# First-block modulation by blocks of 128 weight columns in a two-block transformer kernel

## The chip, the cores and the metric

The kernel runs on one core of one Trainium2 chip. The metric is the device time of one execution in microseconds (us); less is better. Engines are called as the profile calls them: PE (TensorE matmuls), PEld (its weight loads), DVE (VectorE), ACT (ScalarE), POOL (GpSimd) and SP (SyncE, which here only issues transfers).

## The reference, cut to what matters

All inputs are float32. The change touches only the modulation at the head of the first block: two vectors (c for the 1024 tokens of x, c_ctx for the 256 tokens of ctx) go through silu and one matrix of 1024 x 3072, and the result scales, shifts and gates.

```python
mod   = silu(c)     @ w_mod + b_mod          # (1, 3072): shift, scale, gate
mod_c = silu(c_ctx) @ w_mod + b_mod
h  = rms(x,   norm_g) * (1 + scale)   + shift      # 1024 x 1024
hc = rms(ctx, norm_g) * (1 + scale_c) + shift_c    #  256 x 1024
u  = h @ w_in;  uc = hc @ w_in    # parts: cq (256), ckv (128), kr (64), ga, pin, gp (512 each)
...                               # attention, pooling, gates
x = x + gate * (branches @ w_out)
```

The second block (retention and gated linear attention, a dense feed-forward, HGRN2, a mixture of eight experts) follows and is untouched.

## The kernel before

Activations lie transposed, 128 features on the partitions and tokens along the free axis, so the model width of 1024 is eight blocks k. Precise float32 products are made of split operands: a value is a high part `h` (float32r) and a low part `l`, and `mm3` (L214 to L222) issues three matmuls for a product, `wh*xh`, `wh*xl`, `wl*xh`.

Weights come through the class `Weights`. `add` writes an entry into a plan; `get` is called in the order of the plan, loads some entries ahead (`_load`, L108 to L114, one transfer of up to 512 KB into one of four `wraw` buffers, issued on SP or, later, on ACT) and splits up to two ahead (`_split`, L116 to L133: an ACT copy gives `wh`, L130, a DVE subtraction gives `wl`, L131; three pairs of buffers). The order of instructions on each engine is made at build time by a scheduler that goes by the order of the program and by what is ready in its own estimate of time; the engines then run their queues in order.

`first` works in this order. The small vectors are loaded and transposed, silu is taken of c and c_ctx, and `sc` holds the two results split into high and low parts (four columns for each k, L296 to L301). Ten tiles of x and ctx are loaded, transposed on PE (L317) and copied (L320), with their sums of squares (L312); the scale of each token is spread over the partitions by ten float32 products with the identity (L329). Then the modulation: `mod_products` (L372 to L379) takes, for each k and each of the parts shift and scale, the 128 rows of w_mod that belong to k (4 KB in a row, 512 KB in all), with `sc` as the stationary operand (four columns) and the weights moving, 512 columns at a time, high and then low: 64 matmuls into four banks, whose sums are complete only after k = 7. `modulation` (L381 to L396) copies the four rows out (L387), turns them into columns with 16 small transposes (L390) and adds the bias. Only then can the loop over k at L347 start. For each k DVE and ACT make the operands `hch`, `hcl`, `hxh`, `hxl` (L353 to L355) and PE adds the products of this k for ckv and kr: 18 matmuls in six open banks, called a dense step below. After k = 7 ACT drains the banks (L361) and `prep` goes on with cq and pin.

The third part (gate) is taken later, in `branches`: after each of four projections `gp` (48 matmuls each) come the products of two k (8 matmuls each pair of k, 32 in all), and after the last, `modulation` and a copy to `modg` (L689). Attention follows.

Of the kernel before, what the change touches and what calls it, by code (L numbers as in the profile page):

```python
# [10 lines left out]
F32 = mybir.dt.float32  # L11
F32R = mybir.dt.float32r
I32 = mybir.dt.int32
U8 = mybir.dt.uint8
AF = mybir.ActivationFunctionType
OP = mybir.AluOpType
# [5 lines left out]
D = 1024  # L22
NK = 8
HALF = 512
# [70 lines left out]
class Weights:  # L95
# [7 lines left out]
        self.plan, self.loaded, self.ready = [], [], []  # L103
        self.at = 0

    def add(self, key, src, k, m, dup=False):
        self.plan.append((key, src, k, m, dup))

    def _load(self, i):
        key, src, k, m, dup = self.plan[i]  # L110
        t = self.raw.tile([128, 1024], F32, name="wraw", tag="wraw")
        v = t[:, :k * m].rearrange("p (k m) -> p k m", k=k)
        self.queue.dma_start(v, src)
        self.loaded.append(v)  # L114

    def _split(self, i):  # L116
        key, src, k, m, dup = self.plan[i]
        v = self.loaded[i]
        w = 2 * m if dup else m
        h = self.pair.tile([128, 1024], F32R, name="wh", tag="wh")  # L120
        l = self.pair.tile([128, 1024], F32R, name="wl", tag="wl")
        hv = h[:, :k * w].rearrange("p (k m) -> p k m", k=k)
        lv = l[:, :k * w].rearrange("p (k m) -> p k m", k=k)
        if dup:
            for s in range(2):
                self.nc.scalar.activation(hv[:, :, s * m:(s + 1) * m], v, AF.Copy)
                self.nc.vector.tensor_tensor(lv[:, :, s * m:(s + 1) * m], v,
                                             hv[:, :, s * m:(s + 1) * m].bitcast(F32), op=OP.subtract)
        else:
            self.nc.scalar.activation(h[:, :k * w], self._flat(v, k, m), AF.Copy)  # L130
            self.nc.vector.tensor_tensor(l[:, :k * w], self._flat(v, k, m), h[:, :k * w].bitcast(F32),  # L131
                                         op=OP.subtract)
        self.loaded[i] = None  # L133
        self.ready.append((hv, lv))
# [33 lines left out]
OFF_CQ, OFF_CKV, OFF_KR, OFF_GA, OFF_PIN, OFF_GP = 0, 256, 384, 448, 960, 1472  # L168


def wsrc(ap, c0, m, k=NK, r0=0):

    row = ap.shape[-1]
    return bass.AP(tensor=ap.tensor, offset=ap.offset + r0 * row + c0, ap=[[row, 128], [128 * row, k], [1, m]])


class Net:
# [74 lines left out]
    def first(s, stop=99):  # L252
        nc, tc, A = s.nc, s.tc, s.A
        s.vectors()
        W = s.W
        wmod, win, wout = A["w_mod"], A["w_in"], A["w_out"]
        def mod_rows(part, k):
            row = wmod.shape[-1]
            W.add(("mod", part, k), bass.AP(tensor=wmod.tensor, offset=wmod.offset + k * 128 * row + part * D,
                                            ap=[[row, 128], [D, 1], [1, D]]), 1, D)  # L260

        for k in range(NK):
            for part in range(2):
                mod_rows(part, k)
        for key, c0, m, dup in (("ckv", OFF_CKV, 128, False), ("kr", OFF_KR, 64, True), ("cq0", 0, 128, False),
                                ("cq1", 128, 128, False)):
            W.add(key, wsrc(win, c0, m), NK, m, dup)
        for nm, off in (("pin", OFF_PIN), ("ga", OFF_GA), ("gp", OFF_GP)):
            for t in range(4):
                W.add((nm, t), wsrc(win, off + t * 128, 128), NK, 128)  # L270
                if nm == "gp":
                    for k in range(2 * t, 2 * t + 2):
                        mod_rows(2, k)
        for t in range(NK):
            W.add(("wout", t), wsrc(wout, t * 128, 128), NK, 128)

# [2 lines left out]
        ckv = early.tile([128, LK], F32, name="ckv")  # L279
        krr = early.tile([128, LK], F32, name="krr")  # L280
        s.modg = s.const.tile([128, NK], F32, name="modg")
        s.sc = s.const.tile([128, NK, 4], F32R, name="sc")
        st = s.pool("start")
        hch = st.tile([128, NK, CTX], F32R, name="hch")
        hcl = st.tile([128, NK, CTX], F32R, name="hcl")
# [7 lines left out]

        cc = s.vt[:, VCOL["c"]:VCOL["c"] + 16].rearrange("p (v k) -> p v k", v=2)

        sl = st.tile([128, 2, NK], F32, name="sl")  # L296
        silu = nc.scalar.activation(sl, cc, AF.Silu)
        s.lnexp(silu.ins)
        scv = s.sc.rearrange("p k (v q) -> p q v k", q=2)
        nc.vector.tensor_copy(scv[:, 0], sl)  # L300
        nc.vector.tensor_tensor(scv[:, 1], sl, scv[:, 0].bitcast(F32), op=OP.subtract)  # L301

        def psS():
            return s.psS.tile([128, HALF], F32, name="s", tag="s")
# [3 lines left out]
        for i in range(10):  # L308
            xr = rp.tile([128, D], F32, name=f"xr{i}")
            src = A["x"][0, i * 128:(i + 1) * 128, :] if i < 8 else A["ctx"][0, (i - 8) * 128:(i - 7) * 128, :]  # L310
            nc.sync.dma_start(xr, src)
            nc.scalar.activation(junk, xr, AF.Square, accum_out=ss[:, i:i + 1])  # L312
            for g in range(2):
                ps = psS()
                for j in range(4):
                    k = g * 4 + j
# [9 lines left out]
        for a, b in ((0, 4), (4, 8), (8, 10)):  # L326
            ps = psS()
            for i in range(a, b):
# [2 lines left out]
            nc.scalar.activation(rb[:, a * 128:b * 128], ps[:, :(b - a) * 128], AF.Copy)  # L331


        acc = s.mod_banks(s.psA, 2)
        s.mod_products(acc, 0, 2, 2, range(NK))
        mod = s.modulation(st, acc, 0, 2, 2)
        A1 = st.tile([128, NK, 2], F32, name="A1")
        nc.vector.scalar_tensor_tensor(A1, mod[:, NK:], 1.0, s.col("norm_g", 0, 8)[:, :, None].to_broadcast([128, NK, 2]),
                                       op0=OP.add, op1=OP.mult)

        nx = ((0, HALF, hxh, hxl, 0, CTX), (1, HALF, hxh, hxl, HALF, CTX + HALF), (2, CTX, hch, hcl, 0, 0))
        todo = []
        for key, dst, pool, nm in (("ckv", ckv, s.psA, "acc"), ("kr", krr, s.psS, "s")):
            w = W.get(key)
            todo += [(w, dst, p, pool.tile([128, HALF], F32, name=nm, tag=nm)) for p in nx]  # L347
        for k in range(NK):
            for src, v, o, dh, dl in ((cT, 1, T, hch, hcl), (xT, 0, 0, hxh, hxl)):
                a1, sh = A1[:, k, v:v + 1], mod[:, k, v:v + 1]  # L350
                n = src.shape[2]
                t = st.tile([128, T], F32, name="xn", tag="xn", bufs=2)[:, :n]
                nc.vector.scalar_tensor_tensor(t, src[:, k, :], a1, rb[:, o:o + n], op0=OP.mult, op1=OP.mult)  # L353
                nc.scalar.activation(dh[:, k, :], t, AF.Identity, bias=sh)
                nc.vector.scalar_tensor_tensor(dl[:, k, :], t, sh, dh[:, k, :].bitcast(F32), op0=OP.add,  # L355
                                               op1=OP.subtract)
            for w, dst, (i, n, xh, xl, o, d0), ps in todo:
                s.mm3(ps[:, :n], w, lambda k: xh[:, k, o:o + n], lambda k: xl[:, k, o:o + n], (k,), first=k == 0,
                      last=k == NK - 1)
# [4 lines left out]
        st.release()  # L364
        s.prep(hxh, hxl, ckv, krr, early, hxp, stop)


    def mod_banks(s, pool, n):
        nm = "acc" if pool is s.psA else "s"
        return [pool.tile([128, HALF], F32, name=nm, tag=nm) for _ in range(2 * n)]  # L370

    def mod_products(s, acc, part, n, nv, kk):  # L372
        for k in kk:
            for j in range(n):
                for i, w in enumerate(s.W.get(("mod", part + j, k))):
                    for h in range(2):
                        s.nc.tensor.matmul(acc[2 * j + h][:2 * nv], s.sc[:, k, :2 * nv],
                                           w[:, 0, h * HALF:(h + 1) * HALF], start=k == 0 and i == 0,
                                           stop=k == NK - 1 and i == 1)  # L379

    def modulation(s, pool, acc, part, n, nv):  # L381

        nc = s.nc
        ps = s.psS.tile([128, HALF], F32, name="s", tag="s")
        for j in range(2 * n):
            rows = pool.tile([4, HALF], F32, name="mrow", tag="mrow", bufs=2)[:2 * nv]
            nc.vector.tensor_copy(rows, acc[j][:2 * nv])  # L387
            for i in range(4):
                o = (j * 4 + i) * 2 * nv
                nc.tensor.transpose(ps[:, o:o + 2 * nv], rows[:, i * 128:(i + 1) * 128], s.ident[:2 * nv, :2 * nv])  # L390
        mod = pool.tile([128, n * NK, nv], F32, name="mod")
        pv = ps[:, :n * NK * 2 * nv].rearrange("p (j v q) -> p j v q", v=nv, q=2)
        nc.vector.tensor_tensor(mod, pv[:, :, :, 0],
                                s.col("b_mod", part * NK, n * NK)[:, :, None].to_broadcast([128, n * NK, nv]), op=OP.add)
        nc.vector.tensor_tensor(mod, pv[:, :, :, 1], mod, op=OP.add)
        return mod  # L396

    def spill(s):
        return s.spp.tile([128, HALF], F32, name="sp", tag="sp", bufs=4)
# [211 lines left out]
    def branches(s, hxh, hxl, hxp, stop):  # L611

        nc, A = s.nc, s.A
        last = s.rs.ins
        bp = s.pool("pool", side="right")
# [66 lines left out]
        s.heads = {}  # L682
        s.apool = [s.pool("attna")]
        s.load_head(0)
        acc = s.mod_banks(s.psS, 1)
        for t in range(4):
            drain(s.proj([("gp", t)], hxh, hxl, lambda i, hf, ps: evac_gp(t, hf, ps)))
            s.mod_products(acc, 2, 1, 1, range(2 * t, 2 * t + 2))
        nc.vector.tensor_copy(s.modg, s.modulation(bp, acc, 2, 1, 1)[:, :, 0])  # L689
        bp.release()  # L690
        hxp.release()
        s.attention(stop)
# [1698 lines left out]
```

## Time and profile before

| | us |
|---|---|
| median of 3 runs | 4607.41 |
| lowest and highest of them | 4606.77, 4609.05 |
| profiled execution, device time | 4609.74 |
| its span, first to last instruction | 4607.9 |
| busy in the span: PE, PEld, DVE, ACT | 4512.7, 3952.9, 2616.4, 1955.9 |

The profile comes from one execution, 2.3 us above the median. Its busy times are unions of spans of instructions; matmuls are pipelined and their ends are modelled, so a difference of starts tells what one costs, and a duration does not. PEclk is the granted clock of TensorE: 1.00 is 2.4 GHz and 0.50 is 1.2 GHz. A view of waits names the engine that waited and what ended the wait.

### The profile page before, as it was taken

To read this page: it belongs to the slowest core of one execution; us is meant where nothing else is said; L and a number is where in the kernel's file an instruction comes from. 1 tells how busy PE (TensorE), PEld (TensorE's weight loads), DVE (VectorE), ACT (ScalarE), POOL (GpSimd) and SP (SyncE) were. 2 spreads that over 40 slices of the span, in tenths; PEclk is the share of its full clock that TensorE was granted. 3 is DMA by queue.
4 is the path that set the end of the run, shared out by engine and by line. 5 is a ranking of instruction groups with operands and counts; after the bars stand their busy time and mean duration, and the time that the engine had idled before them with its cause. 6 is when DMAs were issued, how large, how long until landed. Compare 5 with 4: busy or idle time off the path is not lost. (4 is left out here: it accounts for less than half of the span.)

```text
span 4607.9 us, 67951 instructions
## 1 busy us (share of the span) xinstructions
PE 4512.7 (98%) x28009; PEld 3952.9 (86%) x28010; DVE 2616.4 (57%) x4271; ACT 1955.9 (42%) x3084; POOL 92.2 (2%) x105
## 2 busy tenths in 40 slices
PE   8999999999999999999999899999999999999999
PEld 5668878787888888888886799999999998989897
DVE  6767765666433333577784564545555465655464
ACT  5654543423211111456663344444444444444463
POOL 0001000000000000000000000000000000000000
PEclk9999999999999999999999899999999999999999
DMA  6466231113311111311114555555555555555583
GB/s 218 166 214 162 55 123 37 47 51 120 113 51 42 42 53 51 98 40 40 45 52 135 181 175 186 181 175 184 175 190 180 195 186 208 188 207 192 202 302 124
DMA packets 430497, 620.39 MB, mean 135 GB/s; under 512 B 16784, under 2 KB 211472, under 8 KB 429152
## 3 DMA queue, kind: packets, MB, share of 16 engines
q1 hardware_dynamic: 393360, 555.45, 35.6%
q0 software_dynamic: 20832, 48.83, 3.5%
q10 hardware_dynamic: 15984, 11.66, 0.9%
q8 instruction: 222, 3.64, 0.3%
q14 instruction: 99, 0.81, 0.1%
HBM read 543.08 MB, written 72.88 MB: 134 GB/s over the span
## 5 line engine op out<-in xcount | busy, mean ns | idle before, releaser
L227 DVE TENSOR_TENSOR ml<-mraw,mh 128x1024 fp32r<-128x1024 f32 (+1 forms) x704 | 824.2, 1176 | 758.8 <-ACT mh L226 745.2
L226 ACT ACTIVATE mh<-mraw 128x1024 fp32r<-128x1024 f32 (+1 forms) x704 | 718.3, 1021 | 1073.5 <-PE m L221 798.4
L221 PE MATMUL m<-xl,mh 128*128 128x272 f32 (+1 forms) x3584 | 1025.7, 286 | 0.0
L222 PE MATMUL m<-xh,ml 128*128 128x272 f32 (+1 forms) x3584 | 1024.1, 286 | 0.0
L220 PE MATMUL m<-xh,mh 128*128 128x272 f32 (+1 forms) x3584 | 1020.4, 285 | 1.0 <-ACT mh L226 1.0
L220 PEld LDWEIGHTS m<-xh,mh 128*128 128x128 f32 x3584 | 677.6, 189 | 1.6 <-ACT mh L226 1.3
L222 PEld LDWEIGHTS m<-xh,ml 128*128 128x128 f32 x3584 | 677.9, 189 | 0.2
L221 PEld LDWEIGHTS m<-xl,mh 128*128 128x128 f32 x3584 | 674.1, 188 | 0.3
L130 ACT ACTIVATE wh<-wraw 128x1024 fp32r<-128x1024 f32 (+2 forms) x208 | 203.5, 980 | 597.9 <-PE acc L221 561.1
L131 DVE TENSOR_TENSOR wl<-wraw,wh 128x1024 fp32r<-128x1024 f32 (+2 forms) x208 | 233.1, 1123 | 118.2 <-ACT wh L130 115.3
L220 PE MATMUL acc<-f2h,wh 128*128 128x512 f32 x704 | 274.8, 390 | 0.0
L221 PE MATMUL acc<-f2l,wh 128*128 128x512 f32 x704 | 273.9, 389 | 0.0
L222 PE MATMUL acc<-f2h,wl 128*128 128x512 f32 x704 | 273.9, 389 | 0.0
L220 PE MATMUL m<-hh,mh 128*128 128x272 f32 x896 | 261.0, 291 | 0.0
L222 PE MATMUL m<-hh,ml 128*128 128x272 f32 x896 | 259.9, 290 | 0.0
L221 PE MATMUL m<-hl,mh 128*128 128x272 f32 x896 | 258.9, 289 | 0.0
L2021 PE MATMUL m<-mh,hh 128*128 128x512 f32 x448 | 177.5, 396 | 0.0
L2023 PE MATMUL m<-mh,hl 128*128 128x512 f32 x448 | 177.0, 395 | 0.0
L2022 PE MATMUL m<-ml,hh 128*128 128x512 f32 x448 | 176.5, 394 | 0.0
L220 PEld LDWEIGHTS m<-hh,mh 128*128 128x128 f32 x896 | 168.6, 188 | 0.4
L221 PEld LDWEIGHTS m<-hl,mh 128*128 128x128 f32 x896 | 168.8, 188 | 0.1
L222 PEld LDWEIGHTS m<-hh,ml 128*128 128x128 f32 x896 | 168.5, 188 | 0.2
(559 smaller groups left out, 8940.4 us busy)
## 6 DMA issues: line engine op xcount, KB each, us to landing
mraw<-in_moe_w_up_dram SPq DMA_DIRECT2D x56, 2048.0 KB, 8.6
mraw<-in_moe_w_down_dram SPq DMA_DIRECT2D x64, 1792.0 KB, 7.6
mraw<-in_moe_w_gate_dram SPq DMA_DIRECT2D x55, 2048.0 KB, 8.6
wraw<-in_c_w_in_dram SPq DMA_DIRECT2D x32, 512.0 KB, 4.0
wraw<-in_ab_w_in_dram SPq DMA_DIRECT2D x28, 512.0 KB, 3.9
xk<-xres SPq DMA_DIRECT2D x24, 512.0 KB, 4.5
wraw<-in_ffn_w_gate_dram SPq DMA_DIRECT2D x22, 512.0 KB, 4.2
wraw<-in_ffn_w_up_dram SPq DMA_DIRECT2D x22, 512.0 KB, 3.8
```

Of the source, the lines that this page charges most:

```text
L130: self.nc.scalar.activation(h[:, :k * w], self._flat(v, k, m), AF.Copy)
L131: self.nc.vector.tensor_tensor(l[:, :k * w], self._flat(v, k, m), h[:, :k * w].bitcast(F32), op=OP.subtract)
L220: mm(ps, wh[:, k, :], xh(k), start=first and i == 0, stop=False)
L221: mm(ps, wh[:, k, :], xl(k), start=False, stop=False)
L222: mm(ps, wl[:, k, :], xh(k), start=False, stop=last and i == n - 1)
L226: s.nc.scalar.activation(h, x, AF.Copy)
L227: s.nc.vector.tensor_tensor(l, x, h.bitcast(F32), op=OP.subtract)
L2021: mm(ac[g], xh, wh, start=f == 0, stop=False)
L2022: mm(ac[g], xh, wl, start=False, stop=False)
L2023: mm(ac[g], xl, wh, start=False, stop=f == NFT - 1)
```

## The change

w_mod is loaded by blocks of 128 columns (eight k side by side, 512 KB as before, now in pieces of 512 bytes) and goes to PE as it is: `raw` entries of the plan are neither copied by ACT nor subtracted by DVE. The weights are the stationary operand and silu(c), in float32 and two columns, moves. A block of shift or scale is complete after its own eight matmuls, already as a column, and needs no transposes. The two blocks of a k are followed by the bias, the operands of that k and its dense step; `operands(k + 1)` stands before the dense step of k in the program. ckv and kr move to the front of the plan. The gate part is taken in the same way behind the projections gp. `sc` is no longer split, and `mod_banks` and `modulation` go.

```diff
+    def add(self, key, src, k, m, dup=False, raw=False):
...
     def _split(self, i):
+        key, src, k, m, dup, raw = self.plan[i]
         v = self.loaded[i]
+        if raw:
+            self.loaded[i] = None
+            self.ready.append(v)
+            return
...
-        for k in range(NK):
-            for part in range(2):
-                mod_rows(part, k)
...
+        def mod_columns(part, j):
+            W.add(("mod", part, j), wsrc(wmod, part * D + j * 128, 128), NK, 128, raw=True)
...
+        proj_columns("ckv", OFF_CKV, 128)
+        proj_columns("kr", OFF_KR, 64, True)
+        for j in range(NK):
+            for part in range(2):
+                mod_columns(part, j)
+        proj_columns("cq0", 0, 128)
+        proj_columns("cq1", 128, 128)
...
-        s.sc = s.const.tile([128, NK, 4], F32R, name="sc")
+        s.sc = s.const.tile([128, NK, 2], F32, name="sc")
...
-        acc = s.mod_banks(s.psA, 2)
-        s.mod_products(acc, 0, 2, 2, range(NK))
-        mod = s.modulation(st, acc, 0, 2, 2)
...
-        for k in range(NK):
+        def operands(k):
+            pool, nm = (s.psA, "acc") if k % 2 == 0 else (s.psS, "s")
+            ps = pool.tile([128, HALF], F32, name=nm, tag=nm)
+            for part in range(2):
+                s.mod_products(ps[:, 2 * part:2 * part + 2], part, k)
+            nc.vector.tensor_tensor(mod[:, k], ps[:, :4].rearrange("p (q v) -> p q v", q=2),
+                                    bias[:, :, k:k + 1].to_broadcast([128, 2, 2]), op=OP.add)
+            nc.vector.scalar_tensor_tensor(A1[:, k], mod[:, k, 1], 1.0, s.col("norm_g", k).to_broadcast([128, 2]),
+                                           op0=OP.add, op1=OP.mult)
             for src, v, o, dh, dl in ((cT, 1, T, hch, hcl), (xT, 0, 0, hxh, hxl)):
...
+        operands(0)
+        for k in range(NK):
+            if k + 1 < NK:
+                operands(k + 1)
             for w, dst, (i, n, xh, xl, o, d0), ps in todo:
                 s.mm3(ps[:, :n], w, lambda k: xh[:, k, o:o + n], lambda k: xl[:, k, o:o + n], (k,), first=k == 0,
                       last=k == NK - 1)
...
+    def mod_products(s, ps, part, j):
+
+        w = s.W.get(("mod", part, j))
+        for k in range(NK):
+            s.nc.tensor.matmul(ps, w[:, k, :], s.sc[:, k, :], start=k == 0, stop=k == NK - 1)
...
-        acc = s.mod_banks(s.psS, 1)
+        mg = s.psS.tile([128, HALF], F32, name="s", tag="s")
         for t in range(4):
             drain(s.proj([("gp", t)], hxh, hxl, lambda i, hf, ps: evac_gp(t, hf, ps)))
-            s.mod_products(acc, 2, 1, 1, range(2 * t, 2 * t + 2))
-        nc.vector.tensor_copy(s.modg, s.modulation(bp, acc, 2, 1, 1)[:, :, 0])
+            for j in range(2 * t, 2 * t + 2):
+                s.mod_products(mg[:, 2 * j:2 * j + 2], 2, j)
+        nc.vector.tensor_tensor(s.modg, mg[:, :2 * NK].rearrange("p (j v) -> p j v", v=2)[:, :, 0],
+                                s.col("b_mod", 2 * NK, NK), op=OP.add)
```

## Rows read from the trace of the kernel before

**Rows 1.** The page, busy time, share of the span and instructions of each engine.

```profile
PE 4512.7 (98%) x28009; PEld 3952.9 (86%) x28010; DVE 2616.4 (57%) x4271; ACT 1955.9 (42%) x3084; POOL 92.2 (2%) x105
```

**Rows 2.** Stretches: length, busy PE, PEld, DVE, ACT, POOL, then PEclk, DMA share, GB/s.

```profile
22.00:63.40 41.40, 27.34 (x106) 12.97 (x106) 31.57 (x39) 22.82 (x28) 0.00 (x0) 0.79 0.87 274
25.80:29.20 3.40, 3.40 (x19) 3.38 (x17) 1.61 (x2) 1.14 (x2) 0.00 (x0) 0.50 0.82 228
39.50:42.80 3.30, 2.97 (x8) 0.67 (x7) 3.17 (x3) 2.34 (x3) 0.00 (x0) 0.50 0.77 226
53.20:63.30 10.10, 5.95 (x20) 4.71 (x21) 8.84 (x15) 3.60 (x5) 0.00 (x0) 0.50 1.10 357
63.40:88.80 25.40, 25.40 (x133) 21.70 (x132) 19.71 (x24) 9.87 (x14) 0.00 (x0) 1.00 0.27 103
88.80:280.00 191.20, 191.19 (x721) 130.58 (x720) 138.45 (x229) 123.80 (x228) 0.00 (x0) 1.00 0.48 164
280.00:370.00 90.00, 78.07 (x318) 58.30 (x318) 51.28 (x58) 32.03 (x42) 11.24 (x16) 0.92 0.81 242
```

**Rows 3.** Waits in 22 to 64 us: who waited for whom, total, times, longest.

```profile
PEld acc L377 <- DVE wl L131: 9.6, 11, 1.7
ACT wh L130 <- DMA wraw<-in_w_mod_dram: 6.6, 7, 1.9
PE acc L220 <- ACT hxh L354: 4.0, 1, 4.0
```

**Rows 4.** A group by line in 22 to 64 us: busy, mean ns, idle before.

```profile
L377 PE MATMUL acc<-wh,sc 128*4 128x512 f32 x28 | 9.6, 427 | 3.1 <-ACT wh L130 3.0
```

**Rows 5.** First matmuls of two successive dense steps (start, length); copies behind the steps.

```profile
64.43 0.39 PE L220 MATMUL acc<-hxh,wh 128*128 128x512 f32 x1
...
67.91 0.39 PE L220 MATMUL acc<-hxh,wh 128*128 128x512 f32 x1
...
L361 ACT ACTIVATE ckv<-acc x3: 385/590/599, 87.5 to 91.5; 128x512 f32<-128x512 f32 x2, 128x256 f32<-128x256 f32 x1
```

**Rows 6.** Line 1712 (eight float32 calls, two moving columns), and its timeline at 2548.70 us.

```profile
L1712 PEld LDWEIGHTS pl<-ones,acc x16: 186/192/192, 2545.6 to 2549.5; 128*128 128x128 f32 x16
L1712 PE MATMUL pl<-ones,acc x16: 167/251/272, 2545.9 to 2549.5; 128*128 128x2 f32 x16
...
2548.70 0.97 PEld L1712 LDWEIGHTS pl<-ones,acc 128*128 128x128 f32 x8
```

**Rows 7.** Line 1039 (float32, two moving columns): timeline, then two stretches around it.

```profile
663.50 0.85 PEld L1039 LDWEIGHTS s<-ident,f1r 128*128 128x128 f32 x6 [5.02 <-DVE f1r L933]
664.08 0.78 PE L1039 MATMUL s<-ident,f1r 128*128 128x2 f32 x3
...
663.50:664.05 0.55, 0.55 (x5) 0.55 (x6) 0.55 (x2) 0.00 (x0) 0.00 (x0) 1.00 0.00 0
664.10:670.90 6.80, 6.80 (x25) 4.00 (x25) 6.80 (x18) 0.00 (x0) 0.00 (x0) 0.50 0.00 0
```

**Rows 8.** Projections gp and their end: PE waits in 280 to 420 us, PE's timeline.

```profile
PE acc L220 <- ACT wh L130: 4.5, 2, 3.6
PE s L390 <- DVE mrow L387: 2.8, 2, 2.7
...
358.77 0.62 PE L377 MATMUL s<-wh,sc 128*2 128x512 f32 x2
359.23 0.63 PE L377 MATMUL s<-wl,sc 128*2 128x512 f32 x2
...
363.45 0.59 PE L744 MATMUL sc<-kn,qn 128*128 128x512 f32 x1
```

**Rows 9.** A stretch with loads of w_in (512-byte pieces); the last number is GB/s.

```profile
48.00:52.00 4.00, 1.61 (x9) 0.44 (x7) 4.00 (x5) 2.34 (x4) 0.00 (x0) 1.00 0.76 180
```

**Rows 10.** Transfers into wraw in 0 to 80 us and in 240 to 420 us: issue to landing.

```profile
DMA to landing us min/median/max: 3.6/5.1/10.2
DMA to landing us min/median/max: 3.4/9.4/20.5
```

More of the change, by code (lines that the diff above doesn't have):

```diff
@@ L104, in __init__ @@
         self.at = 0
-    def add(self, key, src, k, m, dup=False):
-        self.plan.append((key, src, k, m, dup))
+    def add(self, key, src, k, m, dup=False, raw=False):
+        self.plan.append((key, src, k, m, dup, raw))
     def _load(self, i):
-        key, src, k, m, dup = self.plan[i]
+        key, src, k, m, dup, raw = self.plan[i]
         t = self.raw.tile([128, 1024], F32, name="wraw", tag="wraw")
@@ L116, in _split @@
     def _split(self, i):
-        key, src, k, m, dup = self.plan[i]
+        key, src, k, m, dup, raw = self.plan[i]
         v = self.loaded[i]
+        if raw:
+            self.loaded[i] = None
+            self.ready.append(v)
+            return
         w = 2 * m if dup else m
@@ L256, in first, with proj_columns @@
         wmod, win, wout = A["w_mod"], A["w_in"], A["w_out"]
[L257 to L260, printed above, removed]
-        for k in range(NK):
+        def mod_columns(part, j):
+            W.add(("mod", part, j), wsrc(wmod, part * D + j * 128, 128), NK, 128, raw=True)
+        def proj_columns(key, c0, m, dup=False):
+            W.add(key, wsrc(win, c0, m), NK, m, dup)
+        proj_columns("ckv", OFF_CKV, 128)
+        proj_columns("kr", OFF_KR, 64, True)
+        for j in range(NK):
             for part in range(2):
-                mod_rows(part, k)
-        for key, c0, m, dup in (("ckv", OFF_CKV, 128, False), ("kr", OFF_KR, 64, True), ("cq0", 0, 128, False),
-                                ("cq1", 128, 128, False)):
-            W.add(key, wsrc(win, c0, m), NK, m, dup)
+                mod_columns(part, j)
+        proj_columns("cq0", 0, 128)
+        proj_columns("cq1", 128, 128)
         for nm, off in (("pin", OFF_PIN), ("ga", OFF_GA), ("gp", OFF_GP)):
@@ L272, in first @@
                     for k in range(2 * t, 2 * t + 2):
-                        mod_rows(2, k)
+                        mod_columns(2, k)
         for t in range(NK):
@@ L294, in first @@
         cc = s.vt[:, VCOL["c"]:VCOL["c"] + 16].rearrange("p (v k) -> p v k", v=2)
-        sl = st.tile([128, 2, NK], F32, name="sl")
-        silu = nc.scalar.activation(sl, cc, AF.Silu)
+        silu = nc.scalar.activation(s.sc.rearrange("p k v -> p v k"), cc, AF.Silu)
         s.lnexp(silu.ins)
-        scv = s.sc.rearrange("p k (v q) -> p q v k", q=2)
-        nc.vector.tensor_copy(scv[:, 0], sl)
-        nc.vector.tensor_tensor(scv[:, 1], sl, scv[:, 0].bitcast(F32), op=OP.subtract)
         def psS():
@@ L331, in first @@
             nc.scalar.activation(rb[:, a * 128:b * 128], ps[:, :(b - a) * 128], AF.Copy)
-        acc = s.mod_banks(s.psA, 2)
-        s.mod_products(acc, 0, 2, 2, range(NK))
-        mod = s.modulation(st, acc, 0, 2, 2)
-        A1 = st.tile([128, NK, 2], F32, name="A1")
-        nc.vector.scalar_tensor_tensor(A1, mod[:, NK:], 1.0, s.col("norm_g", 0, 8)[:, :, None].to_broadcast([128, NK, 2]),
-                                       op0=OP.add, op1=OP.mult)
         nx = ((0, HALF, hxh, hxl, 0, CTX), (1, HALF, hxh, hxl, HALF, CTX + HALF), (2, CTX, hch, hcl, 0, 0))
@@ L347, in first @@
             todo += [(w, dst, p, pool.tile([128, HALF], F32, name=nm, tag=nm)) for p in nx]
-        for k in range(NK):
+        mod = st.tile([128, NK, 2, 2], F32, name="mod")
+        A1 = st.tile([128, NK, 2], F32, name="A1")
+        bias = s.col("b_mod", 0, 2 * NK).rearrange("p (q k) -> p q k", q=2)
+        def operands(k):
[7 more added lines that the diff above has]
+                                           op0=OP.add, op1=OP.mult)
             for src, v, o, dh, dl in ((cT, 1, T, hch, hcl), (xT, 0, 0, hxh, hxl)):
-                a1, sh = A1[:, k, v:v + 1], mod[:, k, v:v + 1]
+                a1, sh = A1[:, k, v:v + 1], mod[:, k, 0, v:v + 1]
                 n = src.shape[2]
@@ L365, in first @@
         s.prep(hxh, hxl, ckv, krr, early, hxp, stop)
[L368 to L396, printed above, removed]
+    def mod_products(s, ps, part, j):
+        w = s.W.get(("mod", part, j))
+        for k in range(NK):
+            s.nc.tensor.matmul(ps, w[:, k, :], s.sc[:, k, :], start=k == 0, stop=k == NK - 1)
     def spill(s):
```

## The prediction

> **What bounds the kernel now.** The page's engine line comes first: PE is busy for 98% of the span [rows 1], so the question is where the other 2% lie and whether the change touches them. The view by stretches answers [rows 2]. From 22.0 to 63.4 us PE is busy for 27.34 of 41.40 us, 14.1 us idle, and the mean clock is 0.79. From 63.4 to 280 us it is busy without a gap (25.40 of 25.40, 191.19 of 191.20) at 1.00. So whatever brings the work that stands finished at 63.4 us earlier or later moves everything up to 280 us by as much. From 280 to 370 us, where the gate part lies, it is busy for 78.07 of 90 us. The waits of the first stretch say what PE lacked: the low parts of the weights from DVE for 9.6 us, ACT in turn the transfers of w_mod for 6.6, and at the end 4.0 us for the first operand [rows 3]. The stage is a chain of load, copy, subtraction and matmul; the dense steps wait behind all of it.
>
> **What one new matmul costs.** The kernel before has the same form elsewhere: 128 stationary float32 columns, two moving ones. Line 1712 makes eight such calls and the trace has 16 weight loads and 16 matmuls [rows 6]: a call is two passes, each with its own load. Eight loads last 0.97 us in all and one 0.192, so a pass costs (0.97 - 0.192) / 7 = 0.111 us at 2.4 GHz. At 1.2 GHz three matmuls of this form take 0.78 us, one 0.353, so a pass is (0.78 - 0.353) / 2 = 0.214 us [rows 7]. The old product, 512 moving columns behind four or two stationary ones, costs 358.77 to 359.23 for two, 0.23 us [rows 8]. A float32r weight on the new side would have had to be split; here it isn't, but PE pays.
>
> The Trainium skill, page "FP8 and Floating Point Precision", section "TensorE Precision Notes", says that true float32 takes four passes through the array. The two loads and two matmuls of a call [rows 6] speak for two; four stay as a rival below.
>
> **First stage.** Of PE's 27.34 busy us, 3.40 + 2.97 + 5.95 = 12.3 were at half clock [rows 2] and would have been 6.2 at the full one. Gone: the old products (28 with high parts in this stretch [rows 4], as many with low ones), their transposes, ACT copies, DVE subtractions and nearly all of the 14.1 us of idle time. What stays by 63.4 us, at 2.4 GHz: the 20 passes of L329, some 2.2 us (17 of their loads fill the half-clock stretch 25.8 to 29.2, 0.2 us each [rows 2]), and 2.2 us of dense work (some 4.4 of the 5.95 us at half clock just before 63.3). New: 2 parts x 8 blocks x 8 calls = 128 calls, 256 passes x 0.111 = 28.4 us. Together 32.8 us. New idle time: the chain of the first k (bias, A1, operands) takes about the 4.0 us that PE waited for it before [rows 3]; the products of k = 1, 32 passes or 3.6 us, lie in it, and I leave 1.0 us. So without any half clock the point comes 32.8 + 1.0 - 41.4 = -7.6 us earlier.
>
> DVE and ACT don't take over: DVE's 19.71 busy us of 63.4 to 88.8 make some six k, at most 4.2 us for one [rows 2], and PE needs 3.48 us for a dense step [rows 5] and 3.6 for two blocks, 7.1 in all. Transfers neither: a k is 1 MB, 5.8 us at the lowest rate that a stretch with 512-byte pieces shows (180 GB/s [rows 9]). SP gets the 16 loads in the same queue with as many issues; ahead of them now stand ckv and kr, whose splits find ACT and DVE where two splits of w_mod were. The stores of xT wait behind the loads as before.
>
> **The clock.** A pass with two moving columns is a weight load with almost no matmul. Line 1039 shows what that does: after 5.0 us of idle time five passes at 1.00, then the clock falls among them and stays at 0.50 for 6.8 us though PE is busy for 6.80 of 6.80 us, with such passes among 512-column matmuls [rows 7]. So I expect groups of 32 of them (3.6 us) between dense steps to drop the clock. The shortest stretches at 0.50 here last about 3.4 us, others 6.8 and 10.1 [rows 2, 7]; 3.4 us of work at half rate cost 1.7. I take one such stretch for each of eight groups, 13.6 us: near the shortest, because the dense step behind each group is what brought the clock back at 63.3 us. Bounds: none, 0, and all passes at 0.214, 256 x 0.103 = +26.4. First stage: -7.6 + 13.6 = +6.0 us, from -7.6 to +18.8.
>
> **Gate part.** PE has no slack there in the projections: 8 blocks x 8 calls = 128 passes, 14.2 us, for 32 x 0.23 = 7.4, so +6.8. The two copies and eight transposes at the end go: from the last product at 359.23 + 0.46 to attention at 363.45 is 3.8 us [rows 8], one DVE addition stays, -3.3. The clock: three of the four groups with a stretch of 1.7 us, +5.1 (0 to 128 x 0.103 = 13.2). The 3.6 us that PE waits for the last gp weights [rows 8] I leave: their load now waits for a wraw buffer until PE has used it and not until DVE has, so it starts later, and PE comes later too; -3.6 to +3.6. Sum +8.6, from -0.1 to +20.3.
>
> **Sum.** +6.0 + 8.6 = +14.6 us. The profiled execution spans 4607.9 us and took 4609.74, 2.3 above the median 4607.41. On its own time that gives 4624.3; on the median 4622.
>
> **Rivals.** (1) The clock holds. If the scheduler mixes passes and dense matmuls finely, 512-column matmuls are never far apart. Then -7.6 + 3.5 (6.8 - 3.3) = -4.1, 4603; with the wait for gp filled by the longer products 4600. It decides if 22 to 90 us is granted over 0.95. For it: the old stage had only 41% (3.4 + 3.4 + 10.1 of 41.4 us [rows 2]) of its time at half clock. Against it: [rows 7], and program order puts whole groups ahead of a dense step. This one ends on the faster side. (2) Products run ahead of the dense steps, since only weights and a bank hold them: the passes are then all cold, +18.8 + 6.8 - 3.3 + 13.2 = +35.5, 4643, up to 4647 with the wait for gp grown. It needs the weights to land faster than DVE makes operands. (3) The loads bind: each of four buffers is free only after its passes. 16 loads, 4 under way, at the worst landing of the early stretch, 10.2 us, are 41 us and hidden; at the 20.5 of the later one [rows 10], 82 us from 20 us on: the last block would land at 102 and the dense steps end at 107 instead of 63.4 + 8 x 3.48 - 2.2 = 89, first stage +18, all in all +26.6, 4634. (4) A call takes four passes, of which the trace lost two: 384 more x 0.111 = +42.6 us, 4665; [rows 6] with 16 and 16 records for eight calls are against it. It is what the page named above would have.
>
> **Chances.** Forecast 0.52 (4612 to 4634 by one stretch more or less per group), the clock holds 0.22, products ahead and cold 0.14, loads 0.09, four passes 0.03. The range reaches from the warm case with the gp wait filled, 4600, to the cold case, 4643, and leaves the coldest, the four passes and a better mixing out. 0.2% of this time is 9.2 us, about what a measurement can tell from no change. Below 4598.2 lies only a warm clock with more of the gate part hidden than I can show: 0.10. Within: the rest of the warm case (0.12) and the forecast's lower edge (0.14), 0.26. Above: 0.64.
>
> **What would show it.** The products should have 384 weight loads and 384 matmuls, two for each call, with successive starts 0.11 or 0.21 us apart. PE should have no idle time to speak of from 24 to 280 us, DVE and ACT much more. The copies of ckv, 87.5 to 91.5 us before [rows 5], should come about 6 us later. Granted clock: stretches of 0.50 just behind groups of products, with none the first stage ends 7 us earlier. Attention should start 15 us later, with no wait for mrow before it. Were PE idle in 30 to 90 us with SP or a transfer as releaser, rival 3 would be right; a call with four loads would make rival 4 right. If they end earlier than 85 us, my reading of the clock is wrong.

## The result and the profile after

| | kernel before | changed kernel |
|---|---|---|
| median of the runs, us | 4608.71 (7 runs, 4606.04 to 4609.1) | 4633.02 (7 runs, 4615.85 to 4640.07) |
| ratio, 95% interval | | 1.0051, 1.0042 to 1.006 |
| profiled execution, us | 4609.74 | 4629.68 |
| its span, us | 4607.9 | 4627.9 |
| copies of ckv begin, us | 87.5 | 109.0 |
| first product of attention, us | 363.45 | 383.03 |

The change costs 24.3 us between the medians, 20.0 us between the two profiled spans. The second number is there early: the copies of ckv come 21.5 us later and attention 19.6 us later, and the end 20.0 us later. So the loss lies ahead of 109 us. In between the distance is not constant: at the products of line 1712 it is 23.0 us (2568.6 against 2545.6). How far one trace can differ from another without any edit is taken up below. The profiled execution of the changed kernel is the second shortest of its seven.

The page's engine line after, then the view by stretches of the same four as [rows 2] (length, busy PE, PEld, DVE, ACT, POOL, PEclk, DMA share, GB/s):

```profile
PE 4553.4 (98%) x28273; PEld 4010.3 (87%) x28274; DVE 2585.4 (56%) x4250; ACT 1931.9 (42%) x3060; POOL 92.9 (2%) x105
...
22.00:63.40 41.40, 40.80 (x220) 38.14 (x219) 14.79 (x28) 8.35 (x13) 0.00 (x0) 0.67 0.54 150
63.40:88.80 25.40, 25.40 (x111) 23.24 (x110) 7.31 (x14) 2.16 (x3) 0.00 (x0) 0.57 0.37 106
88.80:280.00 191.20, 191.02 (x719) 133.26 (x719) 131.23 (x216) 113.19 (x211) 0.00 (x0) 0.96 0.50 170
280.00:370.00 90.00, 86.85 (x398) 70.66 (x397) 49.77 (x63) 34.54 (x52) 5.85 (x8) 0.94 0.73 228
```

PE is now busy for 40.80 of 41.40 us where it was busy for 27.34 [rows 2]; DVE fell from 31.57 to 14.79 and ACT from 22.82 to 8.35. The chain of load, copy and subtraction is gone, as meant. But PEclk fell from 0.79 to 0.67, and in the next stretch from 1.00 to 0.57. Four stretches of the first stage hold all the half clock, 64.8 us, and PE's records fill them without a gap:

```profile
28.90:39.10 10.20, 10.20 (x40) 9.23 (x40) 5.31 (x9) 3.31 (x4) 0.00 (x0) 0.50 0.67 206
42.60:52.80 10.20, 10.20 (x38) 9.04 (x37) 3.51 (x6) 1.66 (x2) 0.00 (x0) 0.50 0.36 103
56.20:80.10 23.90, 23.90 (x92) 21.87 (x92) 7.14 (x12) 3.81 (x5) 0.00 (x0) 0.50 0.38 110
83.50:104.00 20.50, 20.50 (x75) 18.38 (x75) 8.36 (x13) 3.65 (x4) 0.00 (x0) 0.50 0.45 126
```

In 22 to 87.5 us the kernel before had some 17 us at half clock [rows 2]. PE's timeline around the first fall and rise (start, length, engine, line, operation) shows what stands in such a stretch:

```profile
26.18 1.85 PE L383 MATMUL acc<-sc,wraw 128*128 128x2 f32 x16
27.88 6.05 PE L383 MATMUL s<-sc,wraw 128*128 128x2 f32 x32
33.79 1.20 PE L225 MATMUL acc<-hxh,wh 128*128 128x512 f32 x2
34.79 0.41 PE L225 MATMUL acc<-hch,wh 128*128 128x256 f32 x1
...
38.63 0.63 PE L227 MATMUL s<-hxh,wl 128*128 128x512 f32 x1
39.06 0.44 PE L226 MATMUL s<-hxl,wh 128*128 128x512 f32 x1
39.33 0.40 PE L227 MATMUL s<-hxh,wl 128*128 128x512 f32 x1
...
39.80 4.32 PE L383 MATMUL acc<-sc,wraw 128*128 128x2 f32 x32
```

These are the last 16 passes of the first k, the 32 of the second, and then a dense step with matmuls at 0.63 us that take 0.39 at full clock [rows 5]: the clock falls among the passes (at 28.9), and the dense step behind them pays too, for over 5 us, until it rises at 39.1. The next group follows at once.

The new products by form, in 22 to 115 us (busy us, mean ns); the copies; and the longest waits of DVE in 22 to 110 us:

```profile
L383 PE MATMUL s<-sc,wraw 128*128 128x2 f32 x128 | 24.4, 322 | 0.0
L383 PE MATMUL acc<-sc,wraw 128*128 128x2 f32 x124 | 18.8, 283 | 0.0
...
L373 ACT ACTIVATE ckv<-acc x3: 385/590/597, 109.0 to 112.9; 128x512 f32<-128x512 f32 x2, 128x256 f32<-128x256 f32 x1
...
DVE mod L352 <- PE s L383: 30.0, 4, 9.7
DVE mod L352 <- PE acc L383: 23.9, 4, 7.6
```

(Four of the passes into acc lie ahead of 22 us.) DVE waits for PE, not the other way round. Where the gate part lies, PE waited for DVE's rows and for the last gp weights [rows 8]; neither wait is there after (line numbers moved by the change). PE's longest wait in 280 to 420 us is one for an operand of the pooling (`ph`), which the kernel before has too:

```profile
PE s L225 <- ACT ph L231: 3.1, 2, 2.0
```

### The profile page after: what moved, and what is told of

The parts are those of the page before. It is cut to its first block, busy times and chain, and to the rows that moved or that the text cites. A ratio compares the mean times of both kernels' runs of the same rounds, so it can differ in the third digit from the quotient of the medians.

```text
span 4627.9 us, 68398 instructions
## 1 busy us (share of the span) xinstructions
PE 4553.4 (98%) x28273; PEld 4010.3 (87%) x28274; DVE 2585.4 (56%) x4250; ACT 1931.9 (42%) x3060; POOL 92.9 (2%) x105
## 5 line engine op out<-in xcount | busy, mean ns | idle before, releaser
L135 ACT ACTIVATE wh<-wraw 128x1024 fp32r<-128x1024 f32 (+2 forms) x184 | 178.8, 972 | 577.2 <-PE acc L226 551.7
L136 DVE TENSOR_TENSOR wl<-wraw,wh 128x1024 fp32r<-128x1024 f32 (+2 forms) x184 | 204.3, 1110 | 116.1 <-ACT wh L135 115.0
```

## The experiments

Theory: passes with two moving columns take the clock down, and PE, busy throughout, does all work of the first stage at the lower clock for most of the time. Rivals: the passes are merely many; the loads bind; the long groups, not the narrow passes, are the cause; the gate part is to blame. "Copies" below is the begin of the copies of ckv in a kernel's trace, 87.5 us in the kernel before and 109.0 in the changed one; "half clock" is the time at 0.50 ahead of that.

### One half of the change at a time

**first_only**, the new first stage with the old gate part:

```diff
-                        mod_columns(2, k)
+                        W.add(("mod", 2, k), bass.AP(tensor=wmod.tensor, offset=wmod.offset + k * 128 * 3 * D + 2 * D,
+                                                     ap=[[3 * D, 128], [D, 1], [1, D]]), 1, D)
...
-            for j in range(2 * t, 2 * t + 2):
-                s.mod_products(mg[:, 2 * j:2 * j + 2], 2, j)
+            s.row_products(acc, 2, 1, 1, range(2 * t, 2 * t + 2))
...
```

> The first stage by columns as in the change, the gate part by rows and split as before. If the prediction's terms hold (+6.0 us first stage, +8.6 gate part): 4609 + 6 = 4615 us. If the trace of the changed kernel is read rightly (copies of ckv 21.5 us later, attention only 19.6 us later, so that the gate part gives 2 us back): the median of the changed kernel or a few us above it, 4633 to 4638, and runs spread over some 20 us as the changed kernel's do. Granted clock in 22 to 110 us: 0.5 to 0.7 by the second reading, over 0.8 by the first.

Measured: 4635.03 us (5 runs, 4628.16 to 4640.82), ratio 1.0062 (1.0048 to 1.0075); copies at 110.6, half clock 68.3 us.

**gate_only**, the kernel before with the new gate part:

```diff
-                        mod_rows(2, k)
+                        W.add(("mod", 2, k), wsrc(wmod, 2 * D + k * 128, 128), NK, 128, raw=True)
...
-            s.mod_products(acc, 2, 1, 1, range(2 * t, 2 * t + 2))
+            for j in range(2 * t, 2 * t + 2):
+                s.gate_products(mg[:, 2 * j:2 * j + 2], 2, j)
...
```

> The gate part by columns as in the change, the first stage by rows and split as before. By the prediction +8.6 us: 4617. By the trace of the changed kernel -2 us: 4607, with no wait of PE for the last gp weights (3.6 us before) and attention starting 2 us earlier than 363.45. Runs within 1 to 3 us of each other by both, since the first stage keeps its clock.

Measured: 4615.14 us (11 runs, 4610.78 to 4616.29), ratio 1.0014 (1.0005 to 1.0023); copies at 88.2, half clock 13.7 us. The kernel before, measured beside them, had 4607.5 (27 runs), as for the next two kernels.

So the first stage carries the loss, +27.5 us; with the gate part alone changed the total is 7.6 us longer. The two don't add up: both together have +24.3. The 7.6 us are not spent where the gate part lies: in gate_only's trace, its fastest execution (4610.78), attention begins at 361.42 us, 2.0 earlier than before, as the second reading had it; at line 1712's products the kernel is 4.1 us late (2549.7 against 2545.6) and at the end 1.1. The rest of the 7.6 us shows in no trace. Part of what doesn't add up is also an accident of first_only, seen far from the change. In the mixture of experts PE makes six transposes of gathered rows; the waits ahead of them (total, times, longest) are, in the kernel before and in first_only:

```profile
PE t L1997 <- issue: 6.6, 1, 6.6
```

```profile
PE t L2020 <- issue: 11.7, 2, 6.1
```

"issue" is a wait for nothing that the profile shows. In first_only the six transposes are cut in two by a second wait of 5.6 us; a packet of each of the two queues for instructions falls into it, but that it causes the wait isn't shown. Of all kernels here that take the same experts' work only first_only and wide_old_gate (below) have it, the two that join the new first stage to the old gate part. Without its 5.6 us first_only would stand at about +22, near the +24.3 of both. The rest is within the spread of the first stage (4615.85 to 4640.07 in one kernel); it isn't settled further.

### Holding the clock, with the same passes

**wide_first** repeats the two columns of silu(c) 64 times, so that each call of the first stage moves 128 columns; loads, calls, passes and the order in the program are the same, and 126 of the columns are not used. **wide_both** does so in the gate part too, with 64 columns. PE's own order isn't quite the same, since the scheduler goes by its estimate of time: in wide_first the groups of the last six k stand whole, 32 passes each, and in the changed kernel four of these six are cut into parts of 4 to 22.

```diff
-                s.mod_products(ps[:, 2 * part:2 * part + 2], part, k)
+                s.mod_products(ps[:, 128 * part:128 * part + 128], part, k)
...
-            s.nc.tensor.matmul(ps, w[:, k, :], s.sc[:, k, :], start=k == 0, stop=k == NK - 1)
+            n = ps.shape[1] // 2
+            s.nc.tensor.matmul(ps.rearrange("p (r v) -> p r v", v=2), w[:, k, :],
+                               s.sc[:, k, None, :].to_broadcast([128, n, 2]), start=k == 0, stop=k == NK - 1)
...
```

> The changed kernel, but in the first stage silu(c) moves as 128 columns (its two columns repeated 64 times) and not as two; loads, calls, passes and order of the program are the same, one column pair of each result is used. The row of L332 has 20 passes of this form with 128 moving columns in 2.47 us, about 0.115 us each, as long as one with two columns. If the half clock is the cost: granted clock about 1.00 from 22 to 110 us, copies of ckv at 80 to 86 us, and 28 to 32 us less than the changed kernel, 4601 to 4606. If the loads or the waits for operands are the cost: no change, 4630 or more. If moved columns add to a pass: 256 x 0.107 = +27 us, 4660.

Measured: 4605.4 us (11 runs, 4602.38 to 4608.75), ratio 0.9996 (0.9987 to 1.0005).

```diff
-                s.mod_products(mg[:, 2 * j:2 * j + 2], 2, j)
+                s.mod_products(mg[:, 64 * j:64 * j + 64], 2, j)
...
```

> As the run before it, and in the gate part too, with 64 moving columns (its two columns repeated 32 times). If the clock is the cost there as well, the 10.2 us at 0.50 behind the gate products (349.7 to 360.0 in the changed kernel) go: 5 us less than the run before, 4596 to 4601. If not, the same as the run before.

Measured: 4600.56 us (11 runs, 4599.41 to 4601.72), ratio 0.9984 (0.9975 to 0.9993). It is the fastest kernel of this study, 6.9 us under the kernel before.

The first stage of wide_first, from 22 us to its copies (the columns as in the stretches above), and the copies; below a line of dots, one of its groups of 32 passes:

```profile
22.00:79.40 57.40, 56.49 (x406) 52.22 (x405) 31.92 (x54) 15.86 (x21) 0.00 (x0) 1.00 0.85 247
...
L373 ACT ACTIVATE ckv<-acc x3: 385/590/597, 79.4 to 81.8; 128x512 f32<-128x512 f32 x2, 128x256 f32<-128x256 f32 x1
...
43.00 3.73 PE L384 MATMUL s<-sc,wraw 128*128 128x128 f32 x32
46.49 0.48 PE L225 MATMUL acc<-hxh,wh 128*128 128x512 f32 x1
```

The same stretch of the changed kernel:

```profile
22.00:109.00 87.00, 86.40 (x407) 79.09 (x407) 31.39 (x54) 15.82 (x22) 0.00 (x0) 0.63 0.49 137
```

406 and 407 matmuls, the same work: 57.4 us at a clock of 1.00, 87.0 us at 0.63. A pass that moves 128 columns starts (46.49 - 43.00) / 32 = 0.109 us after the one before, no more than one with two columns [rows 6], so the width is free, and the groups are no shorter than before. That refutes "merely many" and "long groups" as the price of the loss: it is the clock, 109.0 - 79.4 = 29.6 us.

### More and fewer passes

**twice_narrow** makes each call of the first stage a second time, into unused columns of the bank, and **twice_wide** (its diff below) does the same to wide_first:

```diff
-                s.mod_products(ps[:, 2 * part:2 * part + 2], part, k)
+                w = s.W.get(("mod", part, k))
+                for r in range(2):
+                    s.mod_calls(ps[:, 4 * r + 2 * part:4 * r + 2 * part + 2], w)
...
```

> The changed kernel with each call of the first stage made twice, the second time into other columns of the bank: 256 more passes with two moving columns. At 2.4 GHz that is 256 x 0.111 = 28.4 us more (4661), at 1.2 GHz 256 x 0.214 = 54.8 us more (4688). Theory (these passes hold the clock down): +44 to +60 us, 4675 to 4695. Rival (their price is that of the pass alone): 4658 to 4665.

Measured: 4680.4 us (4 runs, 4677.54 to 4688.87), ratio 1.0162 (1.0145 to 1.0179), +47.4 on the changed kernel.

```diff
-                s.mod_products(ps[:, 128 * part:128 * part + 128], part, k)
+                w = s.W.get(("mod", part, k))
+                for r in range(2):
+                    s.mod_calls(ps[:, 256 * r + 128 * part:256 * r + 128 * part + 128], w)
...
```

> The same doubling with 128 moving columns in each call of the first stage: 256 more passes, all at 2.4 GHz if the theory holds, 28.4 us more than the kernel with 128 columns (4605.4): 4631 to 4638 us, no half clock between 22 and 105 us. Rival (a pass with 128 moving columns costs more than one with two, and its cost was hidden by something else): over 4640 us.

Measured: 4634.18 us (4 runs, 4628.66 to 4638.66), ratio 1.0059 (1.0042 to 1.0075), +28.8 on wide_first. The kernel before, measured beside these two and beside mixed_first and few_calls, had 4609.73 (7 runs), 2.2 us more than beside wide_first; set against it, the distance of the two wide kernels is 26.6. The first stage of twice_narrow and of twice_wide:

```profile
22.00:153.50 131.50, 131.42 (x675) 124.37 (x674) 33.15 (x57) 16.72 (x25) 0.00 (x0) 0.64 0.33 96
```

```profile
22.00:107.70 85.70, 84.44 (x661) 80.57 (x660) 32.09 (x54) 16.03 (x22) 0.00 (x0) 1.00 0.57 169
```

With the clock held, 256 more passes cost 107.7 - 79.4 = 28.3 us, 0.111 each: the price of the prediction. Without it they cost 153.5 - 109.0 = 44.5 us, 0.174 each, between the prices at the two clocks.

**few_calls** leaves out seven of the eight calls of each block of shift and scale:

```diff
-                s.mod_products(ps[:, 2 * part:2 * part + 2], part, k)
+                w = s.W.get(("mod", part, k))
+                nc.tensor.matmul(ps[:, 2 * part:2 * part + 2], w[:, k, :], s.sc[:, k, :], start=True, stop=True)
```

> The changed kernel with one call for each block of shift and scale in the first stage in place of eight (the sums over the other seven rows of blocks are left out); all loads, operands and dense steps stay. It takes away 224 of 256 passes, 24.9 us at 2.4 GHz. Theory (PE binds, by passes and clock): the copies of ckv come earlier than the 80 us of the kernel with 128 moving columns, until DVE or the loads bind; 8 MB at 272 GB/s take 31 us, and DVE has 4.2 us for a k against 3.5 of PE: copies at 62 to 72 us, 4582 to 4596 us, with waits of PE for DVE or for transfers. Rival (loads or operands bind already): within 5 us of the kernel with 128 moving columns, 4600 to 4610 us.

Measured: 4704.33 us (4 runs, 4698.9 to 4706.2), ratio 1.0205 (1.0188 to 1.0222). This total says nothing on the first stage: with other activations the tokens go to the experts differently, and the experts' second product grows from 896 to 1344 matmuls with high parts. Read by its trace it answers the question, from 22 us to the copies, and PE's longest waits in 22 to 68 us:

```profile
22.00:63.20 41.20, 35.95 (x187) 30.67 (x188) 30.12 (x53) 15.55 (x23) 0.00 (x0) 0.92 1.06 268
...
PE acc L225 <- ACT hxh L362: 2.8, 1, 2.8
PE s L332 <- DVE r L242: 2.2, 1, 2.2
PE s L352 <- DMA wraw<-in_w_mod_dram: 0.3, 1, 0.3
```

The copies come at 63.2 us, so neither loads nor operands hold the changed kernel at 109 or wide_first at 79.4. PE waits for a transfer of w_mod for 0.3 us in all. 224 passes less gave 16.2 us against wide_first where 24.9 were taken away; 5.2 us of idle time (41.20 - 35.95) and some half clock (6.8 us, here behind an idle PE) took most of the rest.

### The order of the passes

**mixed_first** writes the calls of block k + 1 in threes between the six pieces of dense step k, in place of all ahead of it:

```diff
...
         for k in range(NK):
-            if k + 1 < NK:
-                operands(k + 1)
+            more = products(k + 1) if k + 1 < NK else iter(())
             for w, dst, (i, n, xh, xl, o, d0), ps in todo:
+                for _, nxt in zip(range(3), more):
+                    pass
                 s.mm3(ps[:, :n], w, lambda k: xh[:, k, o:o + n], lambda k: xl[:, k, o:o + n], (k,), first=k == 0,
                       last=k == NK - 1)
+            if k + 1 < NK:
+                operands(k + 1, nxt)
```

> The changed kernel with the 16 calls of block k+1 written in threes between the six pieces of dense step k; passes, loads and moving columns are the same. Theory (a pass with two moving columns keeps the clock down by itself, whatever stands a microsecond away): like the changed kernel, 4622 to 4642 us, with 50 us or more of half clock between 22 and 115 us and the copies of ckv at 105 to 115 us. Rival (the long groups of passes are what costs the clock, my rival 1 of the prediction): the copies at 80 to 90 us, 4603 to 4612 us.

Measured: 4627.3 us (4 runs, 4622.18 to 4636.87), ratio 1.0046 (1.003 to 1.0063); copies at 99.5, half clock 44.4 us in the profiled execution (4623.46). This lay between the two answers, so the same kernel was run again (mixed_again) beside the changed kernel (after_again, without an edit):

> The changed kernel itself once more, beside the two others on the same chip: 4622 to 4640 us, and 40 us or more of half clock before the copies of ckv. It gives the spread of its first stage and stands against the mixed order below.

Measured: 4634.27 us (5 runs, 4633.6 to 4636.99), ratio 1.0058 (1.0044 to 1.0072); copies at 106.8, half clock 58.0 us.

> The mixed order of the first stage once more (calls of block k+1 written in threes between the pieces of dense step k). If the shorter groups keep the clock for longer, its median is 4 to 10 us below that of the changed kernel in this call, and the half clock before the copies shorter by 10 us or more; if the order plays no part, the two medians are within 4 us.

Measured: 4634.64 us (5 runs, 4620.49 to 4637.98), ratio 1.006 (1.0046 to 1.0073). The medians of the two are 0.4 us apart, as if the order played no part. The other sign that I had named came out the other way: in the profiled execution of mixed_again (4620.49, the fastest of its five) the copies come at 99.6 us with 44.4 us of half clock, 13.6 less than in after_again:

```profile
22.00:99.60 77.60, 76.86 (x408) 70.53 (x408) 31.72 (x54) 15.98 (x23) 0.00 (x0) 0.71 0.54 156
```

Three of the nine runs of the mixed order lie under 4625 us, one of the twelve of the changed kernel, so whether the order helps in some executions stays open. It doesn't bring back the 29.6 us: with the copies at 99.5 half clock still takes 44.4 us. And the scheduler put many calls back together, groups of 1 to 16 calls against 2 to 16 in the changed kernel (counted by bank), so a really fine mixture wasn't tried, and rival 1, which speaks of one, was tested only this far.

### The gate part on an undisturbed base

**wide_old_gate** is first_only with the edits of wide_first:

```diff
-                s.mod_products(ps[:, 2 * part:2 * part + 2], part, k)
+                s.mod_products(ps[:, 128 * part:128 * part + 128], part, k)
```

> The new first stage with 128 moving columns, and the gate part as it was in the kernel before (split rows of w_mod, transposes at the end). It gives the first stage without half clock alone, and by its distance from the kernel with 128 columns and the new gate part (4605.4 us) the price of the new gate part on an undisturbed base. By my terms: first stage -7.6, 4607.5 - 7.6 = 4599.9, and 8.6 us under 4605.4 is 4596.8: 4595 to 4601. Rival (the gate part as changed costs nothing, as the trace of the changed kernel has it): 4603 to 4608, as with the new gate part.

Measured: 4608.04 us (11 runs, 4604.02 to 4610.76), ratio 0.9998 (0.9989 to 1.0007); the kernel before had 4608.96 (15 runs). A miss: I expected 4595 to 4601, and the rival's 4603 to 4608 is nearer. Its trace has the gain and loses it again. Against the kernel before it is 8.0 us earlier at the copies (79.5) and 8.9 at attention (354.5), 4.5 at line 1712's products (2541.1 against 2545.6), and 1.1 us later at the first product of the experts (2577.9 against 2576.8), which stands just behind the transposes with the broken wait:

```profile
PE t L2022 <- issue: 12.6, 2, 7.3
```

That is 6.0 us more than the 6.6 of the kernel before, and it lies 2.2 ms behind the gate part. The 4.4 us lost between attention and line 1712 go bit by bit; what costs them isn't shown. So the total says little on the gate part, and the traces are read where it lies, from the copies to attention (columns as in the stretches above). Before, gate_only, changed kernel, wide_first, wide_both:

```profile
87.50:363.40 275.90, 263.96 (x1020) 184.57 (x1018) 186.99 (x280) 155.64 (x270) 6.92 (x10) 0.98 0.58 185
88.20:361.40 273.20, 269.90 (x1108) 196.92 (x1108) 175.28 (x268) 147.21 (x262) 5.87 (x8) 0.98 0.57 184
109.00:383.00 274.00, 270.67 (x1112) 197.56 (x1110) 174.75 (x267) 147.44 (x262) 5.85 (x8) 0.98 0.59 193
79.40:355.80 276.40, 274.06 (x1113) 200.16 (x1113) 174.87 (x268) 147.68 (x262) 5.86 (x8) 0.97 0.56 183
79.50:355.80 276.30, 269.24 (x1115) 195.43 (x1113) 174.87 (x269) 146.30 (x261) 5.87 (x8) 0.99 0.56 182
```

With the new gate part PE is busy for 6 us more in gate_only than in the kernel before, and idle for 3.3 us in place of 11.9. The longer products fill what had been waiting. The three traces with the old gate part take 272.0 to 276.0 us from the copies to attention, the nine with the new one and two moving columns 273.2 to 279.0: a cost of some 2 us between the middle ones (275.0 and 276.9), less than the spread.

wide_both is 4.8 us faster than wide_first (4605.4 - 4600.56), and the two sets of runs don't overlap. But its traces don't put that into the gate part either: PE is busy for 4.8 us less there and idle for 4.7 us more, and attention begins at 355.79 us against 355.82. PE now waits for the last gp weights again:

```profile
PE acc L225 <- ACT wh L135: 2.9, 1, 2.9
```

At line 1712's products wide_both is 1.9 us ahead, at the end 5.7. Most of the difference falls into the mixture of experts, where one stretch at half clock is longer in wide_first than in wide_both. The changed kernel's own two traces, after and after_again, differ there in the same way without any edit. Wide_first, wide_both, after, after_again:

```profile
2547.60:2585.00 37.40, 17.89 (x101) 13.80 (x101) 23.62 (x96) 7.36 (x12) 2.88 (x3) 0.50 0.62 205
2545.30:2575.90 30.60, 11.80 (x78) 9.13 (x79) 21.94 (x96) 6.06 (x9) 2.89 (x3) 0.50 0.61 198
2575.30:2605.90 30.60, 11.73 (x78) 9.06 (x79) 21.43 (x92) 6.05 (x9) 2.89 (x3) 0.50 0.67 218
2577.40:2614.90 37.50, 18.07 (x103) 14.24 (x103) 24.01 (x96) 7.51 (x12) 2.89 (x3) 0.50 0.63 207
```

So the gain of wide_both over wide_first is measured, and its cause is open.

## Why the prediction came out as it did

I predicted 4622, slower by 14.6 us; it was slower by 24.3. The mechanism of the first stage was right and its size was not, and part of the nearness of the total is luck: two terms were wrong in opposite directions. The first stage was to cost 6.0 us and cost 21.5 in the trace, outside its bounds of -7.6 to +18.8; the gate part was to cost 8.6, and from the copies to attention the trace shows -1.9. The two signs that I gave, copies about 6 us later and attention 15 us later, came out as 21.5 and 19.6.

- **What bounds the kernel.** Right. PE was idle for 14.1 us in 22 to 63.4, and is idle for 0.6 now; what it lost in time, it lost while busy.
- **The price of a call.** Right. 256 passes in the first stage and 128 behind gp make two for each of the 192 calls. With two columns 16 of them take 27.88 - 26.18 = 1.70 us at full clock, 0.106 each, and with 128 columns a pass costs 0.111 (twice_wide). Rival 4 needed four. The Trainium skill's page "FP8 and Floating Point Precision", section "TensorE Precision Notes", has four passes for true float32; here the records and the price of the doubling both say two.
- **The first stage without half clock, -7.6 us.** Right: wide_first, which is that case, has its copies 8.1 us earlier. DVE, ACT and the loads stayed out of the way as argued, and rival 3 is refuted by few_calls.
- **The clock, +13.6 us.** This term was mis-sized. It measured 29.6 us (copies at 109.0 against 79.4). I let each of eight groups cost one stretch of 3.4 us, since a dense step had brought the clock back at 63.3 us in the kernel before. The step that failed is that inference from one place: in the changed kernel the first dense step (33.8 to 39.8) ran at 0.50 until 39.1, and later stretches last 20.5 and 23.9 us, over groups and dense steps alike. It also fell outside the bound +26.4, which priced only the passes at the lower clock. Half clock is a price on everything that PE does meanwhile, so the dense work had to be in the bound: 64.8 us of half clock cost at most 32.4. The fall itself I had from line 1039 [rows 7], where five idle microseconds stand just ahead of the passes, so that row could not tell the two apart; wide_first could.
- **The gate part, +8.6 us.** This term was mis-sized too. The total of gate_only, +7.6, is near it, but by luck: where the gate part lies, its trace is 2.7 us shorter than the one before (273.2 against 275.9), and the changed kernel's 1.9 shorter (274.03 against 275.95). The passes cost PE 6 us of busy time there, near the +6.8 of the sum. The step that failed is "PE has no slack there": PE's idle time fell by 8.6 us (11.9 to 3.3), of which I had credited 3.3 and left 3.6 open, and half clock was no dearer than before (mean clock 0.98 in both). Both waits that I looked at went; that for the last gp weights came back when the clock was held (wide_both).
- **The rivals.** Rival 1 gives what the clock decides: 4600 to 4603 if 22 to 90 us are granted over 0.95. The changed kernel had 0.67 and 0.57 there; wide_first and wide_both, with 1.00 up to their copies, came to 4605.4 and 4600.56, though not by the fine mixture that the rival names. In rival 2 the products run ahead of the dense steps and pay the low price throughout. Its time (4643) was as near as my own, but the mechanism wasn't it: the products of the first two k (32 + 32 passes) came ahead, the others stood between pieces of dense steps, and the dense steps paid as well.

## What to carry to other kernels

A matmul with two moving columns had two prices here: 0.111 us for each pass, and what it does to the clock of the work beside it, 29.6 us in all. Before counting passes at the full clock, look in the old trace for a stretch with the same form, and charge half clock to everything that PE runs until the clock rises, not to the new passes alone. Where a pass costs no more with more moving columns (here 0.109 us with 128, 0.111 with two), widening the moving operand with repeats can buy the clock back: here it brought the copies from 109.0 to 79.4 us and the total from 4633.02 to 4605.4, for a few edited lines. Where PE waits for loads anyway, as in the gate part, a faster clock only lengthens the wait. And a total that comes out near its forecast does not show that its terms do: read each term in the trace where it lies.

## What the runs showed of the hardware

- In four stretches, 64.8 us in all, PE's records show no gap and the granted clock was 0.50. The Trainium skill's page "TensorE: Matmul & The Clock Gate", section "Part 1: The HAM clock gate", ties the clock to how busy PE has been of late. The records' busy time doesn't show that here: from 22 us to the copies PE was busy for 86.40 of 87.00 us at 0.63, and with 128 moving columns in place of two for 56.49 of 57.40 at 1.00.
- The changed kernel's runs spread over 24.2 us (4615.85 to 4640.07), wide_both's over 2.3. The mean granted clocks of the changed kernel's fastest and slowest run are 0.988 and 0.983: 0.012 / 0.5 x 4614 = 111 us and 0.017 / 0.5 x 4638 = 158 us at half clock, and half of the difference is 23.5 us. The spread is the clock, as far as three digits tell.
- The same program can differ by 6.9 us of half clock far from any edit: 37.5 and 30.6 us in the mixture of experts (after_again and after). A difference of 3 us between two single traces says nothing there.
- Six transposes in the mixture of experts were cut in two by a wait for nothing shown, 5.6 us in first_only and 5.3 in wide_old_gate, 2.2 ms behind the edited code. That the edit moved it there isn't shown; the two kernels that have it share the new first stage and the old gate part.
